# Roots of the first norm spread over the partitions through DRAM, and query tiles projected ahead of key and value tiles

## The chip, the cores and the metric

The kernel runs on one core of a Trainium2 chip. The metric is device time in microseconds of one execution, the median of several runs. The engines are TensorE (PE: matmuls; PEld: its weight loads), VectorE (DVE), ScalarE (ACT), GpSimd (POOL) and SyncE (SP). DMAs are issued from the queues of SP, ACT and POOL. Each engine works through its instructions in the order in which they were written, and waits for the others at semaphores.

## The reference

One inference step of a decoder layer, for a prompt group of 512 tokens and a sample group of 8 x 4 tokens (544 in all), width 1024:

```python
def _rmsnorm(x, g):
    x32 = x.astype(jnp.float32)
    y = x32 * lax.rsqrt(jnp.mean(x32 * x32, axis=-1, keepdims=True) + EPS) * g.astype(jnp.float32)
...
h = _rmsnorm(x, norm_mix_pre)
proj = h @ w_in                       # x_r | q | k | v | g
xr, q, k, v, g = jnp.split(proj, [c0, c1, c2, c3], axis=-1)
lru_out = _rg_lru(causal_dwconv(xr))
attn = _band_attention(q, k, v)       # window 128, 8 query heads, 2 kv heads, sinks, relative bias
m = (sigmoid(g_lru) * (lru_out @ w_lru_o) + sigmoid(g_attn) * (attn @ w_attn_o)) @ w_out
x = x + _rmsnorm(m, norm_mix_post)
x = x + _rmsnorm(conv_ffn(_rmsnorm(x, norm_ffn_pre)), norm_ffn_post)
```

The scale `rsqrt(mean(x*x) + EPS)` of a token is the same for all its columns, so it can be applied after the projection. The kernel does this: it projects `x * g` and multiplies the result by the token's root.

## The kernel before, in words

Tokens lie along the free axis: a tile holds 128 columns of the model by 544 tokens, in two halves of 256 (`a` = 0) and 288 (`a` = 1) tokens. Every fp32 matmul is made of three: inputs and weights are split into a high and a low part (`hH`, `hL`; `wh_in`, `wl_in`), and high x high, low x high and high x low are added up in PSUM. A pass is one 128-column block of `w_in` by one half of the tokens: 24 matmuls into one of three PSUM banks (`pmin` in the profile; the first pass is `pm_first`). The names `8` to `15` are the blocks of the eight query heads, `16` and `17` those of the two key heads, `18` and `19` those of the values.

`qkv_order` is the order of these blocks. The first five (`FIRST = 5`) make all passes with the first half of the tokens, then all with the second half; the others make both halves in turn. Each pass is a `step`; at its end a `tick` lets generators (`start_at`) emit work that is due, splits the weights of later blocks (`wsplit_hi` on ScalarE, `wsplit_lo` on VectorE), and empties lists of postponed work: `late`, `last`, `mids` (the middle of a pass, ahead of its eight low matmuls) and `after`. The order on PE, ACT, DVE and POOL is thus fixed by the program.

What a pass leaves in PSUM is taken out by `q_done`, `k_done` or `v_done`. A query is only split into high and low (`qH`, `qL`): its root is applied later to the scores, from `rq`, per partition. A key is first multiplied by the root (`scaled`, giving `ks`), then split (`kH`, `kL`); a value is multiplied likewise and later transposed. For these the root of each token has to stand in all 128 partitions: that is the tile `rep`, 128 x 544.

The roots are made from sums of squares in `ss`, where the tokens lie along the partitions: one column for each block of 128 tokens, by `xrstd`. `roots(0, 2)` does the first 256 tokens, `roots(2, 5)` the other 288. Before, the spread from `ss` to `rep` goes over TensorE: VectorE writes diagonal matrices `dg` (identity times the root), TensorE multiplies them by a matrix of ones into `ps_rep`, and ScalarE copies that to `rep`. In the first of these, the same PSUM tile also receives a small product `ohp` x `relx`, the row of relative biases, from which `rvec`, `rscr`, `rrep` and `btab` (the bias tables of the attention) are made by copies through DRAM on POOL's queue.

`hsplit` makes `hH` and `hL` out of the transposed input (`ps_tb` for the second half of the tokens); the passes of the second half read them.

Of the kernel before, what the change touches and what calls it, by code (L numbers as in the profile page):

```python
# [11 lines left out]
F32 = mybir.dt.float32  # L12
F32R = mybir.dt.float32r
AF = mybir.ActivationFunctionType
ALU = mybir.AluOpType
AX = mybir.AxisListType

P = 128
# [6 lines left out]
NT = SEQ + NS  # L25
# [4 lines left out]
NH = 8  # L30
NKV = 2
HD = 128
WIN = 128
# [90 lines left out]
def hawk_step(ctx, tc, I, O):  # L124
    nc = tc.nc
    act, dve, pool, pe = nc.scalar, nc.vector, nc.gpsimd, nc.tensor
# [9 lines left out]
    drp = ctx.enter_context(tc.tile_pool(name="scratch", bufs=1, space=bass.MemoryType.DRAM))  # L136
# [9 lines left out]
    def T(name, dt=F32):  # L146
        return tp.tile([P, FLAT + 4], dt, tag="t", name=name)
# [4 lines left out]
    def PM(name):  # L152
        return psm.tile([P, 512], F32, tag="mm", name=name)

    def PX(name):
        return psx.tile([P, 512], F32, tag="aux", name=name)
# [7 lines left out]
    def mm(out, l, r, start, stop):  # L164
        pe.matmul(out, l, r, start=start, stop=stop)  # L165
# [15 lines left out]
    side, now, serial, late, last, mids, after, taps = [], [0], [0], [], [], [], [], []  # L181
# [5 lines left out]
    def sides():  # L187
        for e in sorted((e for e in side if e[0] <= now[0]), key=lambda e: e[:2]):
            try:
                e[0] = now[0] + (next(e[2]) or 1)  # L190
            except StopIteration:
                side.remove(e)

    def tick(target=0, dt=1):
        now[0] += dt
        todo = late[:]
        late.clear()
        split = [wsplit_hi(u) for u in wclaim(target)]
        tap = taps[:1]
        parts_ = [sides, lambda: [f() for f in todo + tap]]  # L200
        del taps[:1]
        for f in parts_ if now[0] < TURNED else parts_[::-1]:
            f()
        for f in after:
            f()
        after.clear()
        for u in split:
            wsplit_lo(*u)
        for f in last:
            f()  # L210
        last.clear()
# [6 lines left out]
    ones = keep.tile([P, P], F32, name="ones")  # L218
    pool.memset(ones, 1.0)
    ident = keep.tile([P, P], F32, name="ident")  # L220
# [12 lines left out]
        c = key[-1]  # L233
        return w[:, c * P:(c + 1) * P].rearrange("(k p) n -> p k n", p=P)

    qkv_order = (16, 18, 8, 9, 10, 11, 17, 19, 12, 13, 14, 15)
    order = [("in", c) for c in qkv_order]
    pairs = [("in", z + c) for c in range(8) for z in (28, 0)]
    order += pairs[:13] + [("wg", 0)] + pairs[13:]
# [52 lines left out]
    def upto(key, a, look):  # L292
        return 2 * (wpos[key] + look) + a + 1
# [29 lines left out]
    def mmhalf_low_last(ps, key, X, a):  # L323
        wh, wl = ([wunits[2 * wpos[key] + k // 4][j][:, k % 4, :] for k in range(KD)] for j in range(2))
        n = X.half[a][1] - X.half[a][0]
        for k in range(KD):
            mm(ps[:, :n], wh[k], X.get(k, a, 0), k == 0, False)
            mm(ps[:, :n], wh[k], X.get(k, a, 1), False, False)
        for f in mids:
            f()  # L330
        mids.clear()
        for k in range(KD):
            mm(ps[:, :n], wl[k], X.get(k, a, 0), False, k == KD - 1)

    def mmhalf(ps, key, X, a, ks=range(KD)):
        n = X.half[a][1] - X.half[a][0]
        for k in ks:
            wh, wl = (wunits[2 * wpos[key] + k // 4][j][:, k % 4, :] for j in range(2))
            xh, xl = X.get(k, a, 0), X.get(k, a, 1)
            mm(ps[:, :n], wh, xh, k == 0, False)  # L340
            mm(ps[:, :n], wh, xl, False, False)
            mm(ps[:, :n], wl, xh, False, k == KD - 1)

    def step(key, X, a, done, target=None, look=2, quick=False):

        first_ = key == order[0] and a == 0
        ps = first_ps if first_ else PM("pm" + "_".join(str(z) for z in key) + f"_{a}")
        if first_:
            pass
        elif quick:  # L350
            mmhalf(ps, key, X, a, range(4))
            now[0] += 0.5
            sides()
            mmhalf(ps, key, X, a, range(4, 8))
            done(a, ps)
        elif len(wunits) <= 2 * FIRST and a == 0 and key in order[1:FIRST]:
            mmhalf_low_last(ps, key, X, a)
        else:
            mmhalf(ps, key, X, a)
        tick(upto(key, a, look) if target is None else target, 0.5 if quick else 1)  # L360
        if first_:
            after.append(lambda: mids.insert(1, lambda: done(a, ps)))
        elif not quick:
            (last if len(wunits) <= 2 * FIRST and a == 0 else late).append(lambda: done(a, ps))


# [2 lines left out]
    TOK = [(i * P, P, xp[i * P:(i + 1) * P, :]) for i in range(4)] + [(SEQ, NS, xs)]  # L369
# [20 lines left out]
    relx = cp.tile([P, NH], F32, name="relx")  # L390
    pool.memset(relx, 0.0)
    nc.sync.dma_start(out=relx[:NBK, :], in_=I["rel_bias"])
    ohp = T("ohp")[:, 0:WIN]
# [35 lines left out]
    ss = cp.tile([P, 4, 5], F32, name="ss")  # L429
    dve.memset(ss, 1.0)  # L430

    def xsquare(i, z, on_act):
        n = TOK[i][1]
        j_, x_, o_ = T(f"jk{i}_{z}")[:n, 0:512], xt[i, z][:n, 0:512], ss[:n, z, i:i + 1]
        if on_act:
            act.activation(j_, x_, AF.Square, accum_out=o_)
        else:
            dve.scalar_tensor_tensor(out=j_, in0=x_, scalar=1.0, in1=x_, op0=ALU.mult, op1=ALU.mult, accum_out=o_)

    def xsquares(i):  # L440
        xsquare(i, 0, True)
        xsquare(i, 1, False)

    def xrstd(lo, hi):
        c = slice(lo, hi)
        add(ss[:, 0, c], ss[:, 0, c], ss[:, 1, c])
        newton_rstd(ss[:, 1, c], ss[:, 3, c], ss[:, 2, c], ss[:, 0, c])
# [62 lines left out]
    def keep_a(k):  # L510
        act.copy(xn[k][:, 0:256], turned_a(k))
# [9 lines left out]
    rep = cp.tile([P, NT], F32, name="rep")  # L521
    rq = cp.tile([P, 4], F32, name="rq")

    def turn_b(ks):
        tb.extend(PX(f"ps_tb{k}") for k in ks)
        for group in ((2, 3), (4,)):
            for k in ks:
                for i in group:
                    t0, n, _ = TOK[i]
                    pe.transpose(tb[k][:, t0 - 256:t0 - 256 + n], xtile(i, k), ident[:n, :n])  # L530
        for k in ks:
            last.append(lambda k=k, ps=tb[k]: hsplit(k, 1, ps[:, :288]))
        last.extend(lambda k=k, ps=tb[k]: keep_b(k, ps) for k in ks)

    ps_ohp = []

    def roots(i0, i1):
        dg = T(f"dg_{i0}")
        t0 = TOK[i0][0]
        spans = [(TOK[i][0] - t0, TOK[i][1], i) for i in range(i0, i1)]  # L540
        n = spans[-1][0] + spans[-1][1]
        last.append(lambda: xrstd(i0, i1))
        for o, w, i in spans:
            last.append(lambda o=o, w=w, i=i: dve.tensor_scalar(dg[:, o:o + w], ident[:, :w], ss[:, 1, i:i + 1], None,
                                                                ALU.mult))
        yield

        def spread_roots():
            ps = PX(f"ps_rep{i0}")
            mm(ps[:, 0:n], ones, dg[:, 0:n], True, True)  # L550
            if not i0:
                mm(ps[:NH, 256:256 + WIN], relx, ohp, True, True)
                ps_ohp.append(ps)
            act.copy(rep[:, t0:t0 + n], ps[:, 0:n])

        if i0:
            spread_roots()
        else:
            mids.insert(0, spread_roots)

    def norms():
        xsquare(0, 1, True)
        yield from roots(0, 2)
        yield
        last.extend(lambda k=k: keep_a(k) for k in (0, 4, 1, 5, 2, 6))
        last.append(lambda: xsquares(2))
        yield
        turn_b(range(4))
        last.extend(lambda k=k: keep_a(k) for k in (3, 7))
        yield  # L570
        turn_b(range(4, KD))
        last.extend(lambda i=i: xsquares(i) for i in (3, 4))
        yield
        yield from roots(2, 5)
        dve.tensor_scalar(rq, ss[:, 1, 0:4], SCALE, None, ALU.mult)
# [506 lines left out]
    for z, c in enumerate(qkv_order[:FIRST]):  # L1082
        step(("in", c), h, 0, in_done(c), target=2 * z + 4 if z + 2 <= FIRST else 2 * FIRST)
    for z, c in enumerate(qkv_order[:FIRST]):
        step(("in", c), h, 1, in_done(c), target=2 * FIRST + (0, 2, 4, 6, 6)[z])
# [714 lines left out]
    for i, x in enumerate(plan):  # L1800
# [8 lines left out]
        else:  # L1809
            _, q, c, a = x  # L1810
# [104 lines left out]
    def tokens(i, kk):  # L1915
        ps = PM(f"ptok{i}_{kk}")
        t = slice(i * P, (i + 1) * P)
        for k in range(CH):
            wh, wl = (usplit["dl", k, kk][j].rearrange("p k n -> p (k n)") for j in range(2))
            fh, fl = (F.t[QL * CH + k][j][:, t] for j in range(2))  # L1920
            mm(ps, fh, wh, k == 0, False)
            mm(ps, fl, wh, False, False)
            mm(ps, fh, wl, False, k == CH - 1)
        return ps
# [68 lines left out]
    for i, kk in ((0, 0), (0, 1), (1, 0)):  # L1993
        ps = tokens(i, kk)
# [15 lines left out]
    o = ends(0)  # L2010
# [5 lines left out]
    o = ends(1)  # L2016
# [45 lines left out]
```

## Time and profile before

| what | value |
|---|---|
| median of 3 runs | 972.03 us (971.7 to 972.34) |
| the profiled execution | 972.46 us |
| its span, first to last instruction | 970.7 us |
| TensorE busy | 960.7 us |
| VectorE busy | 761.6 us |
| ScalarE busy | 550.5 us |
| GpSimd busy | 167.9 us |
| granted TensorE clock, mean | 0.999 |

A row of the timeline gives start, length, engine, line of the kernel, operation, `out<-in`, shapes and how often. Matmuls are pipelined: one of 256 columns is listed with 0.28 us, but the next starts 0.12 us later. In brackets stand the idle time of the engine just before and what ended it. SPq, ACTq and POOLq are the queues that issue DMAs.

### The profile page before, as it was taken

Reading aid. Unit: us, or ns where it says so; the run is one execution under the profiler, and the core shown is the slowest. Engines: PE = TensorE matmul, PEld = TensorE weight load, DVE = VectorE, ACT = ScalarE, POOL = GpSimd, SP = SyncE. Lnnn points to the kernel's source line nnn. Section 1 sums busy time; section 2 is a strip of 40 time slices with the busy share of each in tenths; the row PEclk is TensorE's granted clock in tenths of the full one; section 3 lists DMA queues with packets and bytes.
Section 4 is the critical chain, followed back from the end, with each engine's and each line's share of the span. In section 5 each row is a group of like instructions: output and inputs, shape, how many; then the busy total and the mean of one; then the engine's idle time right before and its main releaser. Section 6 shows DMA issues by size and latency. Waiting matters only on the chain.

```text
span 970.7 us, 20070 instructions
## 1 busy us (share of the span) xinstructions
PE 960.7 (99%) x7598; PEld 952.3 (98%) x7598; DVE 761.6 (78%) x1623; ACT 550.5 (57%) x1342; POOL 167.9 (17%) x282
## 2 busy tenths in 40 slices
PE   9999999999999999999999999999999999999997
PEld 8999999999999999999999999999999999999996
DVE  5778888857858555599967878787888888888886
ACT  6544533467476425566867665555555565656642
POOL 2152000003406231230011110101011111111024
PEclk9999999999999999999999999999999999999999
DMA  7865435532334537236147576767667675858632
GB/s 222 239 216 182 146 92 146 154 106 88 96 99 152 177 107 187 64 106 195 46 108 196 133 182 147 183 153 175 162 160 189 151 192 136 205 132 232 185 136 92
DMA packets 248412, 147.26 MB, mean 152 GB/s; under 512 B 37332, under 2 KB 232796, under 8 KB 248284
## 3 DMA queue, kind: packets, MB, share of 16 engines
q1 hardware_dynamic: 237324, 124.15, 43.4%
q0 software_dynamic: 9696, 19.42, 11.7%
q10 hardware_dynamic: 1296, 2.43, 0.7%
q8 instruction: 59, 0.97, 0.4%
q14 instruction: 37, 0.30, 0.1%
HBM read 118.21 MB, written 16.74 MB: 139 GB/s over the span
## 4 chain that ended last, share of the span: by engine, by line
PE 89%; DVE 6%; ACT 2%; issue 1%; DMA 1%; POOL 0%; DVEq 0%; ACTq 0%; SPq 0%; POOLq 0%
PE pmin L165 20%; PE pux L1529 16%; PE pmdn L165 16%; PE puy L1529 8%; PE pq L1529 6%; PE pmlo L165 5%; PE pmao L165 5%; PE pmout L165 4%; PE puz L1529 4%; PE pg L165 1%; PE pvp L165 1%; PE psc L165 1%; DVE ft L174 0%; DVE wl_e L168 0%; DVE wl_dl L168 0%
## 5 line engine op out<-in xcount | busy, mean ns | idle before, releaser
L165 PE MATMUL pmin<-hH,wh_in 128*128 128x256 f32 (+1 forms) x568 | 163.9, 291 | 0.0
L165 PE MATMUL pmin<-hL,wh_in 128*128 128x256 f32 (+1 forms) x568 | 162.4, 288 | 0.0
L165 PE MATMUL pmin<-hH,wl_in 128*128 128x256 f32 (+1 forms) x568 | 159.1, 288 | 0.0
L165 PE MATMUL pmdn<-fH,wh_dn 128*128 128x256 f32 (+1 forms) x448 | 129.2, 288 | 0.0
L165 PE MATMUL pmdn<-fH,wl_dn 128*128 128x256 f32 (+1 forms) x448 | 129.0, 288 | 0.0
L165 PE MATMUL pmdn<-fL,wh_dn 128*128 128x256 f32 (+1 forms) x448 | 128.9, 288 | 0.0
L165 PEld LDWEIGHTS pmin<-hH,wh_in 128*128 128x128 f32 x568 | 107.2, 189 | 1.2 <-issue 1.0
L165 PEld LDWEIGHTS pmin<-hL,wh_in 128*128 128x128 f32 x568 | 107.2, 189 | 0.1
L165 PEld LDWEIGHTS pmin<-hH,wl_in 128*128 128x128 f32 x568 | 104.7, 188 | 0.2 <-issue 0.2
L177 DVE SCALAR_TENSOR_TENSOR uc<-u,fv,uc 128x560 f32<-128x560 f32 x128 | 102.0, 797 | 1.7 <-ACT uc L1560 1.1
L165 PEld LDWEIGHTS pmdn<-fH,wl_dn 128*128 128x128 f32 x448 | 84.4, 188 | 0.0
L165 PEld LDWEIGHTS pmdn<-fL,wh_dn 128*128 128x128 f32 x448 | 84.3, 188 | 0.1
L165 PEld LDWEIGHTS pmdn<-fH,wh_dn 128*128 128x128 f32 x448 | 84.3, 188 | 0.1
L1657 ACT COPY u<-pux 128x272 f32<-128x272 f32 x52 | 20.1, 387 | 86.5 <-PE pux L1529 86.5
L168 DVE TENSOR_TENSOR u<-puy,u 128x240 f32<-128x240 f32 (+2 forms) x78 | 24.6, 344 | 47.8 <-PE puy L1529 30.7
L174 DVE TENSOR_TENSOR ft<-ft,pmdn 128x256 f32<-128x256 f32 (+1 forms) x104 | 45.1, 434 | 16.4 <-PE pmdn L165 16.4
L283 ACT ACTIVATE wh_in<-raw_in 128x512 fp32r<-128x512 f32 x70 | 42.2, 625 | 19.0 <-issue 10.6
L290 DVE TENSOR_TENSOR wl_in<-raw_in,wh_in 128x512 fp32r<-128x512 f32 x70 | 47.8, 693 | 1.0 <-ACT wh_in L283 1.0
L1560 ACT ACTIVATE uc<-u,fv 128x560 f32<-128x560 f32 x64 | 48.2, 755 | 0.0
L781 ACT ACTIVATE s<-s,st 128x256 f32<-128x256 f32 (+1 forms) x32 | 15.2, 475 | 53.0 <-DVE st L778 45.3
L168 DVE TENSOR_TENSOR wl_dn<-raw_dn,wh_dn 128x512 fp32r<-128x512 f32 x56 | 38.3, 684 | 3.6 <-ACT wh_dn L1478 3.6
L1467 POOL DMA_DIRECT2D raw_up_s<-raw_up_s x26 | 22.4, 862 | 93.5 <-DMA raw_up_s<-raw_up__11280 5.4
(744 smaller groups left out, 3371.1 us busy)
## 6 DMA issues: line engine op xcount, KB each, us to landing
raw_in<-in_w_in_dram SPq DMA_DIRECT2D x35, 512.0 KB
raw_dn<-in_w_down_dram SPq DMA_DIRECT2D x56, 256.0 KB
raw_up_s<-in_w_up_dram SPq DMA_DIRECT2D x25, 512.0 KB
raw_up_s<-raw_up_s POOLq DMA_DIRECT2D x26, 256.0 KB, 4.2
raw_ao<-in_w_attn_o_dram SPq DMA_DIRECT2D x8, 512.0 KB
raw_lo<-in_w_lru_o_dram SPq DMA_DIRECT2D x8, 512.0 KB
raw_out<-in_w_out_dram SPq DMA_DIRECT2D x8, 512.0 KB
pd<-pb SPq DMA_DIRECT2D x12, 256.0 KB
```

The costliest lines, as they stand in the source:

```text
L165: pe.matmul(out, l, r, start=start, stop=stop)
L168: dve.tensor_tensor(out=out, in0=a, in1=b, op=ALU.subtract)
L174: dve.tensor_tensor(out=out, in0=a, in1=b, op=ALU.add)
L177: dve.scalar_tensor_tensor(out=out, in0=a, scalar=s_, in1=b, op0=op0, op1=op1)
L283: act.activation(hl[0], raw, AF.Copy)
L290: (eng or dve).tensor_tensor(out=hl[1], in0=raw, in1=f32(hl[0]), op=ALU.subtract)
L781: act.activation(s3[:, j, :], s3[:, j, :], AF.Exp, bias=ng[:, j:j + 1], accum_out=sm[:, j:j + 1])
L1467: pool.dma_start(out=w["p4"], in_=w["p2"], accum_op=ALU.add)
L1529: pe.matmul(ps[:, :HN], w, x, start=start and k == 0 and i == 0, stop=stop and k == 3 and i == 2, skip_group_check=True)
L1560: act.activation(yt[j][:, 0:FLATU], u[:, 0:FLATU], AF.Copy, scale=fv[:, j:j + 1])
L1657: act.copy(e[nm_], z)
```

## The change

The diagonals, the products by ones and the copies to `rep` are taken out. Instead, POOL's queue writes the roots of up to two token blocks at a time from `ss` into a row `rrow` in DRAM (`put`), and reads that row back into all partitions of `rep`. For the first 256 tokens that is one put and one spread, for the other 288 two puts and one spread. The product for the relative biases stays, in the same place, in a PSUM tile of its own (`ps_ohp`).

The first five blocks become queries 8, 9, 10 and then key 16 and value 18; before they were 16, 18, 8, 9, 10. The rest of the order is the same. The special case that took the first pass out of PSUM late, in the middle of the third pass (it had to wait for the roots), goes.

```diff
-    qkv_order = (16, 18, 8, 9, 10, 11, 17, 19, 12, 13, 14, 15)
+    qkv_order = (8, 9, 10, 16, 18, 11, 17, 19, 12, 13, 14, 15)
...
-        if first_:
-            after.append(lambda: mids.insert(1, lambda: done(a, ps)))
-        elif not quick:
+        if not quick:
             (last if len(wunits) <= 2 * FIRST and a == 0 else late).append(lambda: done(a, ps))
...
+    rrow = drp.tile([1, NT], F32, name="rrow")
+
+    def bias_rows():
+        ps = PX("ps_ohp")
+        mm(ps[:NH, 256:256 + WIN], relx, ohp, True, True)
+        ps_ohp.append(ps)
+
     def roots(i0, i1):
-        dg = T(f"dg_{i0}")
         t0 = TOK[i0][0]
-        spans = [(TOK[i][0] - t0, TOK[i][1], i) for i in range(i0, i1)]
-        n = spans[-1][0] + spans[-1][1]
         last.append(lambda: xrstd(i0, i1))
-        for o, w, i in spans:
-            last.append(lambda o=o, w=w, i=i: dve.tensor_scalar(dg[:, o:o + w], ident[:, :w], ss[:, 1, i:i + 1], None,
-                                                                ALU.mult))
-        yield
-
-        def spread_roots():
-            ps = PX(f"ps_rep{i0}")
-            mm(ps[:, 0:n], ones, dg[:, 0:n], True, True)
-            if not i0:
-                mm(ps[:NH, 256:256 + WIN], relx, ohp, True, True)
-                ps_ohp.append(ps)
-            act.copy(rep[:, t0:t0 + n], ps[:, 0:n])
-
-        if i0:
-            spread_roots()
-        else:
-            mids.insert(0, spread_roots)
+        for i in range(i0, i1, 2):
+            o, w, _ = TOK[i]
+            m = min(2, i1 - i)
+
+            def put(i=i, o=o, w=w, m=m):
+                pool.dma_start(out=rrow[0, o:o + m * w].rearrange("(i p) -> p i", p=w), in_=ss[:w, 1, i:i + m])
+            last.append(put)
+        end = TOK[i1 - 1][0] + TOK[i1 - 1][1]
+        last.append(lambda: pool.dma_start(out=rep[:, t0:end], in_=rrow[0, t0:end].partition_broadcast(P)))
+        yield
 
     def norms():
         xsquare(0, 1, True)
         yield from roots(0, 2)
+        mids.insert(0, bias_rows)
         yield
```

POOL's queue before, from the write of the bias row on (`kout` and `vout` are the last keys and values, on their way to the outputs):

```order
L661 DMA rscr<-rvec 8x384
L686 DMA rrep_294<-rscr 128x768
L692 DMA btab_470<-rrep_294 128x2x256
L686 DMA rrep_295<-rscr 128x768
L692 DMA btab_678<-rrep_295 128x2x256
L732 DMA out_dram<-kout_790 128x128
```

The same place now:

```order
L550 DMA rrow<-ss 128x2x1
L553 DMA rep<-rrow 128x256
L657 DMA rscr<-rvec 8x384
L682 DMA rrep_295<-rscr 128x768
L688 DMA btab_468<-rrep_295 128x2x256
L682 DMA rrep_296<-rscr 128x768
L550 DMA rrow<-ss 128x2x1
L550 DMA rrow<-ss 32x1
L553 DMA rep<-rrow 128x288
L688 DMA btab_669<-rrep_296 128x2x256
```

The first put and spread stand ahead of the bias row, the second two puts and their spread ahead of the second bias table; each spread waits for its puts to land.

VectorE before, at the end of the first half's passes (`xn` is the unscaled input, kept; `qL` takes the low part of a query):

```order
L514 COPY xn_251<-ps_tb_456 128x288
L514 COPY xn_252<-ps_tb_457 128x288
L168 TENSOR_TENSOR qL_535<-pmin_0_421,qH_534 128x256
L177 SCALAR_TENSOR_TENSOR hL_163<-ps_tb_517,pv,hH_162 128x288
L177 SCALAR_TENSOR_TENSOR hL_165<-ps_tb_518,pv,hH_164 128x288
```

The same place now:

```order
L512 COPY xn_251<-ps_tb_454 128x288
L512 COPY xn_252<-ps_tb_455 128x288
L171 TENSOR_TENSOR ks_0_532<-pmin_0_419,rep 128x256
L177 SCALAR_TENSOR_TENSOR hL_163<-ps_tb_515,pv,hH_162 128x288
L177 SCALAR_TENSOR_TENSOR hL_165<-ps_tb_516,pv,hH_164 128x288
```

Here the first reader of `rep` has moved to: the scaling of the key, ahead of the `hL` that the second half's passes read.

## The prediction

> **What bounds the kernel now.** I read the page first: the span, the busy share of each engine, then the chain that ended last.
>
> ```profile
> span 970.7 us, 20070 instructions
> PE 960.7 (99%) x7598; PEld 952.3 (98%) x7598; DVE 761.6 (78%) x1623; ACT 550.5 (57%) x1342; POOL 167.9 (17%) x282
> PE 89%; DVE 6%; ACT 2%; issue 1%; DMA 1%; POOL 0%; DVEq 0%; ACTq 0%; SPq 0%; POOLq 0%
> ```
>
> TensorE is busy 960.7 of 970.7 us and makes 89% of the chain, so a microsecond of TensorE work that disappears should be a microsecond less, unless another engine becomes late for it. The second view is the same chain in order of time over the first 150 us, where the whole change lies.
>
> ```profile
> 12.32 4.73 PE pmin L165 x40
> 17.05 0.75 PE ps_rep L165 x4
> 17.80 4.09 PE pmin L165 x32
> ```
>
> Columns are start, length, what. From 12.32 us on, this stretch of the chain is TensorE without a gap. Forty projection matmuls of 256 columns take 4.73 us, so one takes 0.118. The matmuls into `ps_rep` stand on the chain itself. The third view, the timeline, shows both places one instruction at a time (start, length, engine, line).
>
> ```profile
> 16.77 0.28 PE L165 MATMUL pmin<-hL,wh_in 128*128 128x256 f32 x1
> 16.89 0.59 PE L165 MATMUL ps_rep<-dg,ones 128*128 128x256 f32 x2
> 17.41 0.39 PE L165 MATMUL ps_rep<-ohp,relx 128*8 128x128 f32 x2
> 17.73 1.20 PE L165 MATMUL pmin<-hH,wl_in 128*128 128x256 f32 x8
> 17.84 0.37 ACT L554 COPY rep<-ps_rep 128x256 f32<-128x256 f32 x1 [3.10 <-PE ps_rep L165]
> 18.10 1.15 ACT L283 ACTIVATE wh_in<-raw_in 128x512 fp32r<-128x512 f32 x2
> 18.81 0.36 PE L165 MATMUL pmin<-hH,wh_in 128*128 128x256 f32 x1
> 19.01 0.28 PE L165 MATMUL pmin<-hL,wh_in 128*128 128x256 f32 x1
> ...
> 33.71 0.29 PE L165 MATMUL pmin<-hH,wl_in 128*128 128x288 f32 x1
> 33.98 0.72 PE L165 MATMUL ps_rep<-dg,ones 128*128 128x288 f32 x2
> 34.33 0.51 PE L165 MATMUL pmin<-hH,wh_in 128*128 128x288 f32 x1
> 34.67 0.30 PE L165 MATMUL pmin<-hL,wh_in 128*128 128x288 f32 x1
> 34.71 3.19 PE pmin L165 x24
> ```
>
> The last row is the chain's again: 24 matmuls of 288 columns in 3.19 us, 0.133 each. Matmuls overlap, so I count from start to start.
>
> **The change part by part.**
>
> *First `ps_rep` product, removed.* From the matmul at 16.77 to the one at 19.01 are 2.24 us. Ten steps lie between them (eight low matmuls and two of the next pass), 10 x 0.118 = 1.18; the other 1.06 us belong to `ps_rep`, to the bias matmul on `ohp`, and to what they cause. The bias matmul stays: 17.41 to 17.73, 0.32. The product itself is 16.89 to 17.41, 0.52, which is the lower end. The upper end is 1.06 - 0.32 = 0.74. The 0.22 between them is at the next pass's start at 18.81: its weights are split by ScalarE at 18.10 (first half done about 18.68), because ScalarE stood 3.10 us waiting for `ps_rep` to copy it. That copy goes, so the split comes earlier, and I take 0.70.
>
> *Second `ps_rep` product, removed.* From 33.71 to 34.67 are 0.96 us for two steps of 0.133, that is 0.69 too much. Nothing is left at this place, so 0.69 goes, with little doubt.
>
> *The diagonals and the copies out of PSUM (five VectorE, two ScalarE instructions), removed.* TensorE has no long waits on these engines, so I cost this at nothing beyond the 0.22 above.
>
> *Five DMAs on POOL's queue, added.* Three of them put the roots into a DRAM row, element by element; two spread that row over 128 partitions. They replace the 1.39 us on TensorE by a chain of transfers, and the question is who needs its end. These rows bound it (the POOL rows are issues; the lines with KB give the median us from issue to landing, the min/median/max line is that of all four `rrep` reads and four `btab` reads):
>
> ```profile
> 19.16 0.71 POOL L661 DMA_DIRECT2D rscr<-rvec  x1 [6.67 <-DVE rvec L660]
> 21.68 0.59 POOL L686 DMA_DIRECT2D rrep<-rscr  x1 [1.81 <-DMA rscr<-rvec]
> 26.29 0.75 POOL L692 DMA_DIRECT2D btab<-rrep  x1 [4.02 <-DMA rrep<-rscr]
> out_dram<-kout POOLq DMA_DIRECT2D x1, 64.0 KB, 2.1
> rrep<-rscr POOLq DMA_DIRECT2D x3, 384.0 KB, 4.9
> DMA to landing us min/median/max: 3.3/5.2/7.0
> ```
>
> No DMA of 4-byte elements is in the trace. The nearest write to DRAM is `kout` (128 rows, 2.1 us from issue), the nearest spread is `rrep` (384 KB, 4.9; ours are 128 and 144 KB). I take 2.1 and 4.9, and as the bad end 7.0 for each. A good end below these does not matter, since nobody asks for `rep` that early.
>
> The start and the need of each come from VectorE's and TensorE's timelines:
>
> ```profile
> 13.92 0.36 DVE L177 SCALAR_TENSOR_TENSOR ss<-ss 128x2 f32<-128x2 f32 x2
> 26.34 0.41 DVE L168 TENSOR_TENSOR qL<-pmin,qH 128x256 fp32r<-128x256 f32 x1
> 27.80 1.79 DVE L177 SCALAR_TENSOR_TENSOR hL<-ps_tb,pv,hH 128x288 fp32r<-128x288 f32 x4 [1.04 <-ACT hH L455]
> 29.18 0.29 PE L165 MATMUL pmin<-hL,wh_in 128*128 128x288 f32 x1
> 32.55 0.36 DVE L177 SCALAR_TENSOR_TENSOR ss<-ss 128x3 f32<-128x3 f32 x2
> 43.72 0.46 DVE L168 TENSOR_TENSOR qL<-pmin,qH 128x288 fp32r<-128x288 f32 x1 [1.47 <-ACT qs L712]
> 49.15 0.30 PE L165 MATMUL pmin<-hH,wh_in 128*128 128x288 f32 x1
> 52.34 0.28 PE L165 MATMUL psc<-kH,qH 128*128 128x256 f32 x1
> ```
>
> *First spread.* The roots are ready at 13.92 + 0.36 = 14.28. Put landed 16.4 (bad end 21.3), spread landed 21.3 (bad end 28.3). The first reader is now the key scaling `ks`, in the place where the query's `qL` stands at 26.34. Four `hL` wait behind it on VectorE, of which the second half of the next pass on TensorE reads the first at 29.18. That `hL` is ready at 27.80 + 1.79/4 = 28.25, 0.93 early, and VectorE idles 1.04 before it. `ks` (0.41) may therefore begin at 27.80 - 0.41 = 27.4, and 0.9 later, 28.3, before TensorE notices; with everything 0.70 earlier that is 27.6. So 21.3 is hidden by 6.3 us, the bad end costs 0.7. Cost taken: 0. Behind the waiting spread on POOL stands `rscr<-rvec`, which needs `rvec` and was issued at 19.16; at 16.4 plus an issue of 0.6 POOL is free again, so the bias table is not delayed.
>
> *Second spread.* Roots ready at 32.55 + 0.36 = 32.91. Two puts, the second issued 0.75 later: 33.66; landed 35.8 (bad end 40.7); spread landed 40.7 (bad end 47.7). The reader, `ks` of the second half, stands about where `qL` is at 43.72. Two things on TensorE need it: the pass at 49.15, which I take to reuse its PSUM bank (three banks, three passes later), and the scores at 52.34, which read the key's low part. Shifted by 1.39 and less 0.46 for `ks`, the earlier asks for it at 49.15 - 1.39 - 0.46 = 47.3. Taken value: hidden by 6.6 us. Bad end: 0.4 late. On POOL the second bias table waits behind this spread, moved from 33.12 to some 36.5; it is read only by the next pair of heads, some 30 us later.
>
> *Queries first, keys and values last.* Same matmuls, same number of splits; the transposes of key and value move behind the scores of the third block. Their users, the products with the values, come at 66 us in the trace, some 10 us after. VectorE loses two early scalings and gets them back where it idled 1.04 and 1.47 us (rows above). Cost 0. On SP, four state loads pass between two loads of one score block; I cost that at nothing too, since SP waits more than it issues there.
>
> *Sum:* 0.70 + 0.69 = 1.39. The profiled execution took 972.46 us (970.7 of span), 0.43 above the median of 972.03; 972.46 - 1.39 = 971.07, and from the median 972.03 - 1.39 = 970.6. The ends of the first term give 970.6 to 970.8.
>
> A page speaks against the new transfers: the Trainium skill (SBUF — State Buffer, section SBUF: two separate sides) says that a DMA issued from POOL gets its descriptors from GpSimd, which VectorE locks out of SBUF during operations in its two-port modes. The trace has POOL's issues at 0.59 to 0.75 us beside a busy VectorE, so such a lock is not seen here. If each of the second spread's three issues waited out one VectorE instruction of the longest kind quoted (0.5 us), `rep` would land at 42.2, and the time would still be 970.6.
>
> **The rivals.**
>
> *B, the gain is given back later (972.0).* TensorE later waits for the softmax of the sample group:
>
> ```profile
> PE pst L911 <- DVE ss L789: 0.7, 1, 0.7
> 147.87 4.37 DMA pt<-pd
> ```
>
> The chain runs there through a transfer of 4.37 us and a row of VectorE work, up to about 169 us. If these stand still while TensorE comes 1.39 earlier, that wait grows from 0.7 to 2.1 and nothing is won. Against it: the transfer is itself released by a TensorE pass that ends at 146.5, which moves along.
>
> *C, faster than the sum (969.9).* The same wait vanishes, because VectorE has five instructions less ahead of it: 970.6 - 0.7 = 969.9. For it: its idle times are short. Against it: a hundred microseconds lie between.
>
> *D, the spread is late (slower, 974).* Place: `ks` at the head of the four `hL`. Past 27.6 every microsecond of lateness stops VectorE and then TensorE, and past 27.6 + 1.39 = 29.0 the kernel is slower than before. It needs 14.7 us for put and spread instead of the 7.0 that the rows give, and 7.0 + 7.0 = 14.0 at the worst seen. With 9 us each (18.0, landing at 32.3) the time is 972.0 + 3.3 = 975.3; with 8.5 each, 974.3. For it: weights are loading just then, and 4-byte elements are unknown here.
>
> **How the numbers follow.** 0.2% is 1.94 us, about what a measurement of this kernel tells from no change, so faster means under 970.1. The sum: 0.65. B: 0.12. C: 0.15. D: 0.08. Predicted 970.6. The sum's own range is 970.2 to 971.1, with 0.4 for the scatter of profiled run and median. The range that leaves out 2 in 10 takes in B and C: 969.6 to 972.2. Chances: faster 0.18 (C and a little of the sum's scatter), same 0.75, slower 0.07.
>
> **What would show it.** Right: `ps_rep` gone from TensorE; the gap at 17 us shrunk to the bias matmul's 0.32; the matmul of 52.34 at about 50.95; VectorE waiting for no DMA at its first `ks`; the span near 969.3. Wrong: a wait of VectorE on `rep<-rrow`, puts that take more than 7 us to land, a TensorE wait near 28 or 48 us that names `hL` or `ks`, or TensorE 1.4 us early at 60 us and no longer early at 200.

## Result: 1.0% slower, and the profile after

The changed kernel takes 981.43 us (median of 5 runs, 981.11 to 982.85) against 972.08 us for the kernel before (5 runs, 971.70 to 972.34): a ratio of 1.0102, with a 95% interval of 1.0091 to 1.0112. The prediction was 970.6 us, with a range of 969.6 to 972.2.

The page of the profiled execution (981.28 us) answers to the first rows shown of before:

```profile
span 979.5 us, 20070 instructions
PE 962.0 (98%) x7594; PEld 953.8 (97%) x7594; DVE 760.2 (78%) x1618; ACT 549.2 (56%) x1340; POOL 169.7 (17%) x287
PE 89%; DVE 7%; ACT 2%; issue 1%; DMA 0%; POOL 0%; DVEq 0%; ACTq 0%; POOLq 0%
```

The span has grown by 8.8 us, TensorE's busy time by only 1.3, so TensorE waits. Where it waits is seen in the chain in order of time (start, length, what):

```profile
16.47 0.32 PE ps_ohp L165 x2
16.78 3.98 PE pmin L165 x32
...
44.42 2.82 PE pmin L165 x24
47.24 6.48 issue
53.72 0.47 DVE ks L171
54.19 0.04 issue
54.24 5.69 PE pmin L165 x24
```

The first place went as forecast: at 16.5 us only the bias product is left between the passes. At 47.24 TensorE stops for 7.0 us and then needs 5.69 us for 24 matmuls that take 24 x 0.133 = 3.2. TensorE's waits and POOL's name the cause (what waits, for what; us in total, times, longest):

```profile
PE pmin L165 <- DVE ks L171: 7.0, 1, 7.0
POOL rep L553 <- DMA rrow<-ss: 11.5, 1, 11.5
```

The timeline of POOL and VectorE shows each put, each spread and the two key scalings `ks` (start, length; in brackets the idle time before, and what ended it):

```profile
14.29 0.91 POOL L550 DMA_DIRECT2D rrow<-ss  x1 [2.43 <-ACT wh_in L283]
23.25 0.59 POOL L553 DMA_DIRECT2D rep<-rrow  x1 [8.06 <-DMA rrow<-ss]
27.27 0.42 DVE L171 TENSOR_TENSOR ks<-pmin,rep 128x256 f32<-128x256 f32 x1 [2.37 <-DMA rep<-rrow]
35.02 1.27 POOL L550 DMA_DIRECT2D rrow<-ss  x2
47.83 0.57 POOL L553 DMA_DIRECT2D rep<-rrow  x1 [11.54 <-DMA rrow<-ss]
53.72 0.46 DVE L171 TENSOR_TENSOR ks<-pmin,rep 128x288 f32<-128x288 f32 x1 [10.90 <-issue]
DMA to landing us min/median/max: 4.0/8.7/12.1
```

The last row is that of all transfers on `rrow`. The first put (issued at 14.29) took 8.7 us, so that its spread landed at 27.2, about in time. The second puts (35.02) took 12.1 and 11.5, and their spread could start only at 47.83. VectorE stood 10.9 us at the second `ks`, since 42.8.

A table by stage of the same execution (TensorE busy with its matmuls, granted TensorE clock, busy share of the DMA engines, GB/s) shows two things more:

```profile
38.00:42.00 4.00, 4.00 (x33) 1.00 1.21 241
42.00:46.00 4.00, 4.00 (x34) 1.00 0.98 80
46.00:50.00 4.00, 1.23 (x11) 1.00 0.93 253
50.00:54.00 4.00, 0.00 (x0) 0.80 0.94 321
54.00:58.00 4.00, 3.76 (x15) 0.50 0.25 96
```

While the second puts are under way (42 to 46 us), the DMA engines count as fully busy but move 80 GB/s, where they move 250 to 320 a little later: the puts seem to hold up the weight loads too, which e14 below bears out. And after its stop TensorE is granted half its clock (0.50): 5.69 - 3.19 = 2.5 us more.

How late TensorE is, is best read from one event that every kernel has: the start of each of the 16 blocks of score products (`psc`), against before. Block 2 (45.61 us before) starts 2.06 earlier, block 3 (52.34) 7.42 later, block 10 (104.27) 8.04 later. The loss between blocks 2 and 3 is 9.48 us; the wait (7.00) and the half clock (2.50) add up to 9.50. The 0.6 us lost between blocks 3 and 7 belong to the new order: e3 below, which has nothing else of the change, loses as much there.

### The profile page after: what moved, and what is told of

Read it like the earlier page. It is cut to its first block, busy times and chain, and to the rows that moved or that the text cites. A ratio compares the mean times of both kernels' runs of the same rounds, so it can differ in the third digit from the quotient of the medians.

```text
span 979.5 us, 20070 instructions
## 1 busy us (share of the span) xinstructions
PE 962.0 (98%) x7594; PEld 953.8 (97%) x7594; DVE 760.2 (78%) x1618; ACT 549.2 (56%) x1340; POOL 169.7 (17%) x287
## 4 chain that ended last, share of the span: by engine, by line
PE 89%; DVE 7%; ACT 2%; issue 1%; DMA 0%; POOL 0%; DVEq 0%; ACTq 0%; POOLq 0%
PE pmin L165 20%; PE pux L1525 16%; PE pmdn L165 16%; PE puy L1525 8%; PE pq L1525 6%; PE pmlo L165 5%; PE pmao L165 5%; PE pmout L165 4%; PE puz L1525 4%; PE pg L165 1%; PE pvp L165 1%; PE psc L165 1%; DVE ft L174 0%; DVE wl_e L168 0%; DVE wl_dl L168 0%
```

## The experiments

The same event is used for all. "Lag" is the start of a score block less its start in the kernel before, in us, in the profiled execution; second `ks` is the time at which VectorE starts the second half's key scaling. All these numbers are read from the timelines.

| kernel | time, us | second `ks` | lag at block 3 | at block 7 | at block 10 |
|---|---|---|---|---|---|
| changed kernel | 981.43 | 53.72 | 7.42 | 8.03 | 8.04 |
| e1 first spread by DMA only | 974.75 | 44.96 | 2.42 | 3.01 | 3.76 |
| e2 second spread by DMA only | 981.74 | 51.70 | 4.68 | 5.25 | 7.54 |
| e3 order alone | 972.96 | 41.69 | -0.64 | -0.05 | 0.33 |
| e4 runs of 8 and 12 bytes | 977.23 | 49.13 | 0.81 | 1.85 | 4.00 |
| e5 runs of 128 bytes | 975.45 | 46.67 | -1.85 | -1.05 | 1.57 |
| e6 put to a row in SBUF | 978.18 | 50.98 | 4.94 | 5.56 | 5.78 |
| e7 puts from ScalarE's queue | 985.84 | 58.91 | 11.90 | 12.48 | 13.35 |
| e8 idle products | 985.17 | 56.68 | 8.16 | 8.88 | 11.00 |
| e9 runs of 128 bytes, later `ks` | 972.17 | 46.72 | -2.01 | -1.42 | -0.83 |
| e10 e5's first spread only | 972.22 | 40.74 | -1.61 | -1.02 | -1.04 |
| e11 VectorE held, no DMA | 976.68 | 48.55 | 0.01 | 0.73 | 2.87 |
| e12 half the loads | 980.87 | 52.50 | 6.58 | 7.14 | 7.12 |
| e13 e2 with idle products | 980.97 | 51.87 | 3.34 | 4.02 | 6.31 |

### Which part costs: e1, e2, e3

In e1 the second spread goes back to TensorE, in e2 the first, in e3 both; everything else is the changed kernel (`roots_pe` is `roots` of the kernel before).

```diff
-        yield from roots(0, 2)          # e2, e3
-        mids.insert(0, bias_rows)
+        yield from roots_pe(0, 2)
...
-        yield from roots(2, 5)          # e1, e3
+        yield from roots_pe(2, 5)
```

> As the changed kernel, but the second spread (288 tokens) is made by TensorE again (diagonals, product by ones, copy); the first stays a DMA. Theory S (all of the loss is the second spread, which lands 6.5 us after TensorE needs its pass's bank, and the slower clock behind it): no TensorE wait of 7 us, no 0.50 clock near 54 us; first product's 0.70 gained, up to 0.5 given back because the first key scaling at 27.3 is just late: 971.3 to 971.9. Rival O (the order of queries, keys and values costs something by itself): at least 974, with TensorE waits at other places.

> As the changed kernel, but the first spread (256 tokens) is made by TensorE again; the second stays two puts and a spread by DMA. Theory S: the wait of TensorE on the second key scaling stays at about 7 us and the clock falls behind it: 981.4 + 0.7 for the product that is back - 0.5 = 981.6 (981.0 to 982.3). Rival F (the first put and spread hold up the queue or the weight loads, and so make the second put slow): the second puts land in under 6 us and the time is under 977.

> Only the new order of query, key and value blocks and the end of the special case; both spreads by TensorE as before. Theory S: 972.1 (971.6 to 972.6), no change. Rival O: the order costs 2 us or more (974 and up).

Measured: e1 974.75 us (ratio 1.0034, 1.0021 to 1.0046), e2 981.74 (1.0103, 1.0087 to 1.0118), e3 972.96 (1.0008, 0.9999 to 1.0017). The order alone costs 0.9 us by the medians, which its interval does not tell from nothing. The second spread carries most of the loss: e2 is as slow as the whole change. Its puts took 11.5 and 11.0 us with no DMA for the first spread ahead of them, so rival F falls. But e1 missed: the first spread alone costs 1.8 us over e3, where I had expected 0.7 of gain and at most 0.5 back. Its rows (timeline, then a table by stage as above):

```profile
25.31 0.59 POOL L553 DMA_DIRECT2D rep<-rrow  x1 [9.59 <-DMA rrow<-ss]
30.67 0.40 PE L165 MATMUL pmin<-hL,wh_in 128*128 128x288 f32 x1 [1.98 <-DVE hL L177]
...
29.00:30.00 1.00, 0.00 (x0) 1.00 0.26 28
31.00:32.00 1.00, 1.00 (x9) 0.98 0.91 247
32.00:33.00 1.00, 1.00 (x6) 0.50 0.88 229
34.00:35.00 1.00, 1.00 (x6) 0.50 1.11 340
```

Here the first put took 10.2 us (issued at 14.81), `ks` came at 29.77 and not at 27.27, and TensorE waited 1.98 us for the `hL` behind it. That is rival D at the place where the prediction put it, and the half clock from 32 to 35 us came on top. The changed kernel, with the same instructions up to that point, had the same put done in 8.7 us and got away with it. The profiled execution of e1 was its slowest (976.58 us), so its lag is more than its median has.

### What makes the puts slow: e4, e5, e6, e7, e12

A run of bytes is here a stretch that lies side by side and is written as one piece. In the puts of the change, each root is a run of 4 bytes.

In e4 each partition writes its two or three roots as one run, so a group of tokens is one put of 128 runs:

```diff
+        pool.dma_start(out=rrow[0, c0:c0 + m * P].rearrange("(p i) -> p i", i=m), in_=ss[:, 1, i0:i1])
```

> As the changed kernel, but each partition writes its 2 or 3 roots as one run of 8 or 12 bytes (128 runs, one put for each group of tokens, not 256 and 256 + 32 runs of 4 bytes in one and two puts); rep then holds the roots token by token of a block, and its readers pick them with a stride. Theory E (the put is slow because of its 4-byte elements): both puts land in 2 to 5 us, the wait of 7 us falls to 0 to 2, time 972 to 975. Theory L (whatever is issued at that time is slow, because weight loads fill the DMA engines): second put lands in 9 to 12 us still, the wait stays 5 us or more, time 979 to 982.

Measured: 977.23 us (1.0051, 1.0039 to 1.0064). The puts took 5.3 and 8.9 us:

```profile
DMA to landing us min/median/max: 5.0/5.8/8.9
```

The time lies between the two theories: the form of the runs matters, but the second put still missed its due time.

In e5 VectorE transposes the roots first, so that 32 of them lie on one partition:

```diff
+        last.append(lambda: dve.transpose(t_[:, 32:64], t_[:, 0:32]))
...
+                pool.dma_start(out=rrow[0, o:o + w].rearrange("(b j) -> b j", j=32), in_=t_[i - lo:w:32, 32:64])
```

> As the changed kernel, but VectorE first turns the roots (a 32 x 32 block transpose), so that 32 of them lie in a row on one partition, and the puts write runs of 128 bytes: 8 runs for the first group, 9 for the second, in five puts. Theory E (a put costs some 0.4 us for each small run on each of the 16 DMA engines, and holds up all other loads meanwhile): puts land in 2 to 4 us, no stretch of slow loads behind them, no TensorE wait on a key scaling; time is that of the order alone less the two products, 973.0 - 1.4 = 971.6 (971.0 to 972.3). Rival L (weight loads ahead of the put make it late, whatever its form): second spread lands after 50, time 977 or more.

Measured: 975.45 us (1.0041, 1.0028 to 1.0053). TensorE no longer waits at 47 us, and at block 3 it leads by 1.85 us, more than the 1.4 of the sum. But second `ks` is at 46.67, and the lead is lost between 82 and 105 us. My expectation of 971.6 missed this; the next group of experiments is about it. Three rows, the first of the timeline, the others of TensorE's waits and of the chain:

```profile
46.67 0.46 DVE L171 TENSOR_TENSOR ks<-pmin,rep 128x288 f32<-128x288 f32 x1 [6.74 <-DMA rep<-rrow]
PE pmin L165 <- DVE qL L168: 1.8, 2, 1.4
34.30 6.58 DMA rrow<-rt
```

The 6.58 us are those of the last of three puts at this place, that of the 32 sample tokens. The program writes it as one run of 128 bytes, but its record in the trace has 16 pieces of 8 bytes. The two puts of four runs just ahead of it took 5.4 us each; those of the first group took 5.1 and 4.6.

In e6 the 4-byte runs go to a row in SBUF, from there in one run to DRAM:

```diff
+                pool.dma_start(out=row[0:1, o - t0:o - t0 + w], in_=ss[:w, 1, i:i + 1])
...
+        last.append(lambda: pool.dma_start(out=rrow[:, t0:end], in_=row[0:1, 0:end - t0]))
```

> As the changed kernel, but the 4-byte puts go to a row in SBUF (five puts), from there in one run to the row in DRAM, then the same spread: one hop more. Theory W (small runs are slow because they are writes to DRAM): puts land in 2 to 4 us, loads behind them keep their rate; spread 2 lands near 46 to 49, time 971.5 to 975. Rival N (small runs are slow wherever they go): puts of 8 us and more, loads slowed, the hop on top: 981 to 985.

Measured: 978.18 us (1.0060, 1.0045 to 1.0075), 3.3 less than the change in spite of one more hop, but not the 971.5 to 975 expected. The list of DMA issues (KB, median us from issue to landing):

```profile
row<-ss POOLq DMA_DIRECT2D x4, 0.5 KB, 5.5
rrow<-row POOLq DMA_DIRECT2D x1, 1.1 KB, 3.6
```

Into SBUF the 4-byte pieces, 128 to a put and not 256, took a median of 5.5 us: more than theory W had (2 to 4), less than rival N (8 and more).

In e7 the puts are issued from ScalarE's queue:

```diff
-                pool.dma_start(out=rrow[0, o:o + m * w]
+                act.dma_start(out=rrow[0, o:o + m * w]
```

> As the changed kernel, but the three puts are issued from ScalarE's queue; the two spreads stay on POOL's. Theory E (the runs themselves are slow): puts still 8 to 12 us, loads slowed behind them, 979 to 983. Rival Q (descriptors that POOL's software writes are what is slow): puts land in 2 to 4 us, time 971.5 to 974.

Measured: 985.84 us (1.0145, 1.0131 to 1.0159), slower than either theory said. The first put was issued at 19.58 and its spread at 29.33, so it took about 9.7 us; the second puts were issued at 40.81, their spread 11.5 us later. That POOL's queue issues the puts is not the cause, and rival Q falls. The time on top comes from ScalarE, which was late with the weights, and TensorE waited 3.8 us more for the second `ks`:

```profile
19.58 0.40 ACTq L550 DMA_DIRECT2D rrow<-ss  x1
PE pmin L165 <- ACT wh_in L283: 5.8, 1, 5.8
```

In e12 eight weight blocks are loaded by half, so that the traffic beside the second puts is halved (the products that use them are altered):

```diff
+            if 5 <= i < 13:
+                nc.sync.dma_start(out=raw[:, 0:4, :], in_=wsrc(key)[:, 0:4, :])
```

> The changed kernel, but eight weight blocks (those loaded at 27 to 48 us) are loaded by half and their first half is used twice: this alters the products and halves the traffic beside the second put. Theory E (256 + 32 runs of 4 bytes are slow by themselves): the second put still takes 8 to 10 us (as the first did with idle DMA engines), rep lands near 48.5, time 975 to 978. Rival L (the put waits for the weight loads): it takes 2 to 4 us, rep lands near 42, time 971 to 973.

Measured: 980.87 us (1.0091, 1.0077 to 1.0105), outside both ranges and nearest to the change itself. The spread was issued 11.9 us after the puts (36.33):

```profile
48.20 0.57 POOL L557 DMA_DIRECT2D rep<-rrow  x1 [10.60 <-DMA rrow<-ss]
```

The second put took 11.1 us, where it took 12.1 in the change. So halving the weight loads ahead does not make the 4-byte puts fast. It does not take the other traffic away; e14 has a put without it.

### The price of a put by itself: e14

Six puts that nobody reads are added to the kernel before, about 17 to 30 us apart, on POOL's queue.

```diff
+        go("pa256x4", 256, lambda d: d.rearrange("(i p) -> p i", p=P), two)
+        go("pb128x4", 128, lambda d: d.rearrange("(i p) -> p i", p=P), one)
+        go("pc256x4far", 4096, lambda d: d.rearrange("(i p z) -> p i z", p=P, z=16)[:, :, 0], two)
+        go("pd128x8", 256, lambda d: d.rearrange("(p i) -> p i", i=2), two)
+        go("pe128x64", 2048, lambda d: d.rearrange("(p i) -> p i", i=16), ident[:, 0:16])
+        go("pf256x4", 256, lambda d: d.rearrange("(i p) -> p i", p=P), two)
```

> The kernel before, with six more puts on POOL's queue, some 19 us apart, between about 95 and 200 us; nobody reads them. In turn: 256 runs of 4 bytes side by side (as in the change), 128 runs of 4 bytes side by side, 256 runs of 4 bytes 64 bytes apart, 128 runs of 8 bytes, 128 runs of 64 bytes, and the first once more. Theory E1 (a put pays for each run below some size, wherever it lies): 256 runs of 4 bytes 7 to 10 us both near and far, 128 runs half of that, 64 bytes 2 us. Theory E2 (runs that share a stretch of 64 bytes get in each other's way): near 7 to 10, far 2 to 4, 8 bytes between them. The time itself (972 to 973) tells nothing here.

The list of DMA issues (KB, us from issue to landing), and the table by stage beside the last put, issued at 208.71 (the columns are busy times of PE, PEld, DVE, ACT and POOL, then clock, DMA share and GB/s):

```profile
pc256x4far<-ss POOLq DMA_DIRECT2D x1, 1.0 KB, 4.8
pd128x<-ss POOLq DMA_DIRECT2D x1, 1.0 KB, 6.5
pe128x<-ident POOLq DMA_DIRECT2D x1, 8.0 KB, 4.5
pf256x<-ss POOLq DMA_DIRECT2D x1, 1.0 KB, 11.3
...
215.00:219.00 4.00, 4.00 (x35) 4.00 (x35) 2.79 (x12) 3.74 (x8) 0.00 (x0) 1.00 0.18 30
219.00:223.00 4.00, 4.00 (x32) 4.00 (x32) 2.82 (x6) 0.92 (x2) 0.33 (x2) 1.00 0.61 129
```

256 runs of 4 bytes side by side take 11.3 us (10.3 the first time, at 86.6 us); the same 256 runs, 64 bytes apart, take 4.8. So it is not the number of runs (theory E1): neighbouring runs get in each other's way (E2), though both times are longer than E2 had (7 to 10, and 2 to 4). 128 runs of 8 bytes side by side are between, at 6.5, and 128 runs of 64 bytes, eight times the data, take 4.5. Only the first form was measured twice. Beside the last put the DMA engines were nearly idle, at a busy share of 0.06 from 208 to 210 us, 0.02 and 0.00 in the next two stretches of 2 us: the put takes 11.3 us without other traffic. A weight load that was issued at 214.11 us, behind the last put, moves at 30 GB/s from 215 to 219 us; the put lands at 220, and from 219 to 223 it is 129.

I had written that the time of this kernel tells nothing. It does: 979.27 us in its one run, 6.8 us late at 200 us, from transfers that nobody waits for. The attention's own `pd<-pb`, issued behind the 128 runs of 4 bytes, shows how (SP's queue):

```profile
112.53 0.53 SPq L826 DMA_DIRECT2D pd<-pb  x1
116.41 1.74 SPq L831 DMA_DIRECT2D pt<-pd  x4
...
118.74 0.52 SPq L826 DMA_DIRECT2D pd<-pb  x1
130.66 2.02 SPq L831 DMA_DIRECT2D pt<-pd  x4
```

The read `pt` waits for `pd` to land: 3.9 us after its issue in one block, 11.9 in the next, behind the put.

### Where the loss goes on: e9, e10, e11

e9 is e5 with the second half's key and value taken out of PSUM unscaled by ScalarE; VectorE's scalings stand behind the first softmax and the next scores.

```diff
+            act.copy(t[:, 0:288], ps[:, 0:288])
...
+                mul(t[:, 0:288], t[:, 0:288], rep[:, 256:NT])
...
+            start_at(now[0] + 1, later())
```

> As the kernel with runs of 128 bytes, but for the second half of the first key and value block ScalarE copies PSUM out unscaled at once, and VectorE's two multiplications by the roots stand behind the first softmax and the next scores, about 3 us later in its order. Theory V (VectorE's wait of 6.7 us for the second spread, with the softmax of the first blocks queued behind it, is what that kernel pays for at 83 to 105 us): VectorE's wait falls under 1 us, the lead of TensorE (1.3 us at 58) is kept, time 971.6 (971.0 to 972.3). Rival (the loss at 83 to 105 us comes from the order of transfers on SP, not from VectorE): 974.5 to 976 as before this edit.

Measured: 972.17 us (1.0001, 0.9992 to 1.0010), inside the expected range. The second `ks` starts at the same time as in e5, but VectorE no longer stands waiting for it with the softmax queued behind. (The edit also frees the PSUM bank earlier, by ScalarE's copy. But TensorE does not wait for that bank in e5 either, and at block 3 the two kernels are 0.2 us apart.)

```profile
46.72 0.46 DVE L171 TENSOR_TENSOR ks<-ks,rep 128x288 f32<-128x288 f32 x1 [0.26 <-DMA rep<-rrow]
```

e10 has e5's first spread and TensorE's second (the edits of e5 and e1 together).

> First spread by DMA with runs of 128 bytes, second spread by TensorE. Theory E (the 974.75 of the kernel with only the first spread by DMA came from its 4-byte put, which landed after 10 us): put and spread land by 25.5, no wait on hL; time is the order alone less the first product, 973.0 - 0.7 = 972.3 (971.7 to 972.8). Rival (any DMA spread there costs): 974 or more.

Measured: 972.22 us (1.0001, 0.9992 to 1.0010), against 974.75 for e1: the loss of e1 was its 4-byte put.

e11 is e3 (no DMA for the roots) with nine idle VectorE instructions ahead of the second `ks`:

```diff
+            for z in range(9):
+                stt(idle[:, 0:512], idle[:, 0:512], 1.0, idle[:, 0:512], ALU.mult, ALU.mult)
```

> The new order alone with both spreads by TensorE (973.0), and nine idle VectorE instructions (about 6 us, results unused) ahead of the second half's key scaling: VectorE is late by as much as a late spread makes it, with no DMA in it. Theory V (past about 45 us each us by which VectorE comes to that key scaling late is a us of the kernel): key scaling near 48, time 975.5 to 977. Rival P (only the PSUM bank that TensorE asks for near 48 counts): 973.0 to 973.6.

Measured: 976.68 us (1.0052, 1.0040 to 1.0065), in the range of theory V, and 3.7 more than e3. Lateness of VectorE at this one place costs time without any transfer in it:

```profile
42.12 6.51 DVE L177 SCALAR_TENSOR_TENSOR idle<-idle 128x512 f32<-128x512 f32 x9
48.55 0.45 DVE L171 TENSOR_TENSOR ks<-pmin,rep 128x288 f32<-128x288 f32 x1
```

The table at the head of this section tells more. Take the second `ks` on TensorE's own time, that is, less the lag at block 3. Where this is 45.9 to 46.3 (e12, e6, the changed kernel), the lag grows by 0.2 at most from block 7 to block 10. In e2, e4, e5, e8, e11 and e13 it is 47.0 to 48.5, and the lag grows by 2.1 to 2.6. In these six, and in no other of the table, TensorE stops once for 0.9 to 1.4 us between 84 and 96 us, for a `qL` of VectorE. So it is not one us for each us, as I had put it for e11, but more like a step. Where the step lies is not settled: e7 is at 47.0 too, has no such stop, and grows by 0.9 only. e9, with 48.7 and only 0.6 lost, points to the work behind the wait as what counts.

### The half clock: e8, e13

Idle products keep TensorE at work while it waits, 24 in the changed kernel (e8), 14 in e2 (e13):

```diff
+            if c == 11 and a:
+                pf = PX("ps_fill")
+                for z in range(24):
+                    mm(pf[:, (z % 4) * P:(z % 4 + 1) * P], ones, ones, True, True)
```

> As the changed kernel, with 24 idle products of ones by ones (about 6 us of TensorE, results unused) ahead of the pass that stalls, so that TensorE is not still while it waits. Theory C (2.5 us of the loss are the pass after the wait at half clock, because TensorE stood still): the pass takes 3.2 us instead of 5.7, its clock 1.0; time 981.4 - 2.5 = 978.9 (978.2 to 979.8). Rival: the clock falls anyway or the fill itself costs: 981 or more.

> The kernel with only the second spread by DMA (981.74; TensorE waits 3.9 us for the key scaling and runs at half clock behind it), with 14 idle products of ones by ones (about 3.4 us, results unused) ahead of the pass that stalls. Theory V (VectorE, held until the second spread has landed at 51.6, sets the end; TensorE's wait and its slower clock lie beside that): clock 1.0 behind the fill, TensorE about 2 us earlier at 57 us, and all of that lost again by 105 us: 981.0 to 982.5. Rival C (the slower clock adds about 2 us to the loss): 979.2 to 980.3.

Measured: e8 985.17 us (1.0135, 1.0121 to 1.0149), e13 980.97 (1.0090, 1.0077 to 1.0104). In both the clock stays whole after the fill. The tables by stage of e13 and, below the dots, of e2:

```profile
50.00:54.00 4.00, 2.58 (x21) 1.00 0.72 284
54.00:58.00 4.00, 4.00 (x35) 1.00 0.40 119
...
50.00:54.00 4.00, 1.79 (x11) 0.90 0.85 307
54.00:58.00 4.00, 4.00 (x24) 0.67 0.41 124
```

e8 proves nothing about its worth: its first put took 10.1 us, TensorE waited 2.6 us for `hL` near 30, and everything after came later. In e13 the second `ks` is as in e2. TensorE is 1.3 us earlier at block 3, and still 1.2 at block 10: theory V, which had all of it lost again, is wrong there, and the half clock does add to the loss. The medians differ by 0.8 us, less than the scatter within each (979.99 to 982.22, and 980.66 to 982.62), so how much of it the whole kernel keeps stays open.

## Why the prediction was wrong, point by point

*The two products, 1.39 us.* Right, as far as TensorE goes: the gap at 17 us is the bias product's 0.32, and TensorE is 2.06 us early at 45.6 (0.6 of that has the order alone as well). With runs of 128 bytes and the later scaling (e9) it keeps 0.83 of it at 104 us. The kernel's time then is that of before (972.17), so what is left of the gain is below what these runs tell apart.

*The failed step: "Five DMAs on POOL's queue", the price of a put.* I took 2.1 us from the `kout` row and called 7.0 the bad end. Measured: 8.7 for the first (10.2 in e1), 12.1 and 11.5 for the second. `kout` has 128 runs of 512 bytes; the puts have runs of 4 bytes side by side. I said that none such is in the trace, and still took the longest transfer of a quite different form as their upper end. e14 shows what that form costs (4.8 us apart, 10.3 to 11.3 side by side), and e12 and the last put of e14 that other traffic has little part in it. The Trainium skill (DMA: Bandwidth & Descriptors, section Anatomy of one DMA — SWDGE (gpsimd) path) gives a fit of 2.0 us plus bytes / 436e3 for such a DMA, by which an estimate for 1 KB is about 2.0 us; it would have misled in the same way, and the measurement decides.

The spreads were sized well: 4.0 and 5.8 us against 4.9 taken.

*Due times.* Right: the first `ks` (due at 27.6) started at 27.27 and cost little; the second was due at 47.3, and TensorE stopped at 47.24, on the PSUM bank named. The sum with the measured put would have been 33.66 + 11.5 + 0.6 + 5.8 = 51.6 for the second spread, 4.3 us late.

*POOL's queue, a second step that failed.* The second spread landed at 53.6, 2 us later than even that sum. The prediction had POOL free again an issue of 0.6 after 16.4, and the bias table not delayed. But the write of the bias row stood behind the first spread, which waited for its slow put. It was issued at 23.84 and not at 19.16, the copies behind it came late too, and the second puts stood behind these on POOL. Their roots were ready at 33.05; they were issued at 35.02:

```profile
23.84 0.55 POOL L657 DMA_DIRECT2D rscr<-rvec  x1
33.73 0.74 POOL L688 DMA_DIRECT2D btab<-rrep  x1 [5.45 <-DMA rrep<-rscr]
```

In e2, where the first spread is TensorE's, the second puts are issued at 33.77 and the second `ks` comes at 51.70, as that sum says.

*Rival D (0.08).* The right mechanism. The prediction placed it at the first spread, where it struck in e1 and e8. In the changed kernel it struck at the second, which is priced from the same rows; there the prediction gave it only "0.4 late".

*What was not in any rival.* First, the puts slow the other transfers down (80 GB/s at 42 to 46 us), so the 8 weight loads on SP's queue, 15.92 us of issues before, took 20.34. Second, the half clock after a stop: 2.5 us. Third, VectorE's queue: the prediction asked who waits for the late `ks` on TensorE, and not what is queued behind it on VectorE at the second place. There it is the softmax of the first score blocks. By the medians such lateness is worth 3.3 us in e5 (against e9) and 3.7 in e11 (against e3). In the changed kernel itself it cost nothing that shows (lag 8.03 at block 7, 8.04 at block 10): presumably because TensorE itself had stopped for longer there.

*Queries first, cost 0.* 0.9 us by the medians of e3, not told from nothing; in its profile TensorE leads by 0.64 us at block 3 and is 0.33 behind at block 10. *Rivals B and C.* Where the spread is not late (e9, e10), TensorE still leads by 0.8 to 1.0 us at 200 us, and the wait near 168 us that B and C name is 0.8 us in both (0.7 before), so it takes or gives nothing of what they said; yet the medians are those of before. In the profiled executions of the changed kernel, e5 and e9 TensorE drifts by some 0.6 us against before between 690 and 820 us, in those of e3 and e10 by 0.2 at most. That is not explained here.

## What to carry to other kernels

Before a product on the busy engine is replaced by transfers, price the transfer in its own form: the length of its runs and whether neighbouring runs are written side by side, not its bytes. A put of 256 pieces of 4 bytes side by side into DRAM took 8.7 to 13.1 us here, and the other queues were slowed meanwhile; after a transpose on VectorE that makes runs of 128 bytes, the puts took 4.2 to 6.6. And a wait for a transfer belongs behind the work that does not need it: e5 and e9 have the same transfers, landing at the same time, and differ by 3.3 us through the place of the scalings in VectorE's order, with a copy by ScalarE that lets them stand there.

## What the runs showed of the hardware

256 runs of 4 bytes into DRAM took 10.3 and 11.3 us side by side and 4.8 us at a distance of 64 bytes. Why neighbours hinder each other, and at which distance it ends, was not tried.

A short stop of TensorE brings the half clock. Between 10 and 900 us, every stop of up to 1.90 us (e4, to 49.87) left the clock at 1.00, and every one from 1.98 us on (e1, to 30.67) brought 0.50. It held for 3.4 us (e1, e2, e8, e14) or 6.8 us (the changed kernel, from 52.4 to 59.3; e6; e12), once each in e7, and the length of the stop does not decide which: 3.9 us in e2 gave 3.4, and 4.0 us in e12 gave 6.8. The Trainium skill (TensorE: Matmul & The Clock Gate, section HAM oscillation — how this bites in real kernels) puts the limit for a pause at about 3.4 us; here 2.0 was enough, and in e1 it came 1.3 us after work had begun again.
